# Expert output product in fp32r parts instead of fp32, with two scaled-output buffers

## The chip, the core and the metric

The kernel runs on one core of a Trainium2 chip. The metric is the device time of one execution in microseconds (us). The core has five engines that run side by side, each through its own list of instructions in a fixed order: TensorE (PE in the rows; PEld is its weight load), VectorE (DVE), ScalarE (ACT), GpSimd (POOL) and SyncE (SP), which here only starts transfers. They wait for each other and for DMA transfers by semaphores.

## The reference, cut to what matters

Two layers; each mixes tokens by attention and a recurrent scan, and then sends its 1024 tokens through a mixture of 32 experts, two of them per token:

```python
def block_mlp(args):
    tok, e = args
    xb = h_pad[tok]                                      # up to 128 tokens of expert e
    hid = jax.nn.silu(xb @ w_gate[e]) * (xb @ w_up[e])   # 1024 -> 256
    return hid @ w_down[e]                               # 256 -> 1024: the output product
...
y = jax.ops.segment_sum(yb.reshape(R, D) * row_w[:, None], row_tok, num_segments=T + 1)
```

## The kernel before, in words

Each layer has a mixing part and then the expert loop in `moe`, which handles 35 blocks of 128 rows in turn (32 experts and three slots for experts with more than 128 rows). Only this loop is changed. Each expert e goes through these steps:

- **Gather** (GpSimd, L1614): 128 token rows are fetched by index into one of two `xg`.
- **Prepare** (L1625): TensorE turns the rows in eight transposes into PSUM; ScalarE casts them to `xT_hi` (fp32r), and VectorE subtracts that from the PSUM values, which leaves the second part `xT_lo`.
- **Weights**: SyncE loads the 1 MB halves of `w_gu`, two per expert, into raw buffers (`RAW` of them), and the 1 MB `w_d` into one of three. For each half, `split` (L1591) has ScalarE cast it to `w_hi` and VectorE subtract to get `w_lo`, all 128x2048; three pairs of buffers hold the parts.
- **Up** (L1640): 24 matmuls, for each of eight slices hi x hi, lo x hi and hi x lo, into `h_ps`.
- **Hidden** (L1634): tanh on ScalarE, two VectorE instructions on `th` (128x256).
- **Turned** (L1663): two transposes of `th`, and a ScalarE copy to `hT`.
- **Down** (L1682): the output product in plain fp32, `hT` by `w_d`, four matmuls in the program that run as eight passes on TensorE, into `y_ps`; VectorE scales the result by the token's weight and the gate `gt2` into `yo` (L1673), of which there is one buffer.
- **Scatter** (GpSimd, L1676): `yo` goes by index to rows of `yd` in memory.

`in_order` pins the order of the loop's instructions on TensorE, ScalarE, VectorE and GpSimd to that of the program: in turn e these are `up`(e), the first split of a half, `turned`(e-1), `prepare`(e+1), `gather`(e+3), `hidden`(e), then `down`(e-1), `scatter`(e-1) and the second split. SyncE's loads are issued in program order with waits for the buffers. `route_overflow` (the tables for experts with more rows; `ro_or` on VectorE, `ro_pv` on TensorE) isn't pinned: a scheduler mixes it into the first turns of the loop. Everything else in the program is ordered by the scheduler too.

Of the kernel before, what the change touches and what calls it, by code (L numbers as in the profile page):

```python
# [10 lines left out]
F32 = mybir.dt.float32  # L11
F32R = mybir.dt.float32r
# [3 lines left out]
OP = mybir.AluOpType  # L16
# [4 lines left out]
T = 1024  # L21
D = 1024
# [30 lines left out]
class Trunk:  # L53
# [1516 lines left out]
        self.raw = [wp.tile([128, 4, 512], F32, name=f"w_gu{i}") for i in range(2)]  # L1570
        self.wd = [wp.tile([128, 2, D], F32, name="w_d0")]

    RAW = 5

    def more_tiles(self, wp):
        self.parts = [[wp.tile([128, 4, 512], F32R, name=f"w_{n}{i}") for n in ("hi", "lo")] for i in range(3)]
# [9 lines left out]
        self.nc.sync.dma_start(self.raw[n % self.RAW], self.expert_source(l, e, "moe_w_gu")[n % 2])  # L1586

    def load_d(self, l, i, e):
        self.nc.sync.dma_start(self.wd[i % 3], self.expert_source(l, e, "moe_w_down"))

    def split(self, raw, parts, eng):  # L1591

# [3 lines left out]

    def split_half(self, n, eng=None):
        self.split(self.raw[n % self.RAW], self.parts[n % 3], eng or self.nc.vector)

    def moe(self, l, side, psum):  # L1600

        nc, tc = self.nc, self.tc
        with ExitStack() as s:
            xp, tx = s.enter_context(self.pool(name="xE", bufs=2, side=side)), self.tx
            gt2 = tx.tile([128, D], F32, name="gt2", tag="v2", bufs=1)
# [1 line left out]
            for x in xg:  # L1607
                nc.gpsimd.memset(x, 0.0)
            ths = tx.tile([128, 2, 256], F32, name="th", tag="mt")
            hT = tx.tile([128, 2, 128], F32, name="hT", tag="mt")  # L1610
            scat = []

            def gather(e):
# [11 lines left out]
            def prepare(e):  # L1625

                pt = transposed(e)
                hi = tx.tile([128, 8, 128], F32R, name="xT_hi", tag="hl")
                lo = xp.tile([128, 8, 128], F32R, name="xT_lo", tag="xT_lo")
                nc.scalar.copy(hi, pt)  # L1630
                nc.vector.tensor_tensor(lo, pt, hi.bitcast(F32), op=OP.subtract)  # L1631
                return hi, lo

            def hidden(e, ph):  # L1634
                th = ths[:, e % 2]
                nc.scalar.activation(th, ph[:, 0:256], AF.Tanh, scale=0.5)
                nc.vector.scalar_tensor_tensor(th, th, 1.0, ph[:, 0:256], op0=OP.add, op1=OP.mult)
                nc.vector.tensor_mul(th, th, ph[:, 256:512])
# [21 lines left out]
                    nc.tensor.matmul(ph, x[:, k, :], self.raw[(2 * e + k // 4) % self.RAW][:, k % 4, :], start=(k == 0), stop=(k == NK - 1))  # L1660
                hidden(e, ph)

            def turned(e):  # L1663
                pt = psum.tile([128, 2, 128], F32, name="hT_ps", tag="hT", bufs=1)
                for k in range(2):
                    nc.tensor.transpose(pt[:, k, :], ths[:, e % 2, 128 * k:128 * k + 128], self.ident)
                nc.scalar.copy(hT, pt)

            yos = {}

            def scaled(e, po):
                yo = yos[e] = tx.tile([128, D], F32, name="yo", tag="x", bufs=1)
                nc.vector.scalar_tensor_tensor(yo, po, self.wsl[:, e:e + 1], gt2, op0=OP.mult, op1=OP.mult)  # L1673

            def scatter(e):
                st = nc.gpsimd.indirect_dma_start(out=self.yd, out_offset=bass.IndirectOffsetOnAxis(ap=self.idx_s[:, e:e + 1], axis=0),  # L1676
                                                  in_=yos.pop(e), in_offset=None, bounds_check=2 * T - 1, oob_is_err=False)
                for o in scat:
                    tc.declare_no_dep(st.ins, o.ins, reason="every slot holds another row")
                scat.append(st)  # L1680

            def down(e):  # L1682
                w = self.wd[e % 3]
# [17 lines left out]
            N = 32 + self.MORE_E  # L1701
# [8 lines left out]
            for e in range(N):  # L1710
                with self.in_order(last):
                    ph = up(e, x)
                    if e + 1 < N:
                        self.split_half(2 * e + 3)
                    if e:
                        turned(e - 1)
                    if e + 1 < N:
                        x = prepare(e + 1)
                    if e + 3 < N:
                        gather(e + 3)  # L1720
                    hidden(e, ph)
                if e == 0:
                    nc.sync.dma_start(gt2, self.mod_row(l, 5).partition_broadcast(128))
                with self.in_order(last):
                    if e:
                        down(e - 1)
                        scatter(e - 1)
                    if e + 2 < N:
                        self.split_half(2 * e + 4)
                for n in (2 * e + 8, 2 * e + 9):  # L1730
                    if n < 2 * N:
                        self.load_gu(l, n, expert(n // 2))
                if e and e + 2 < N:
# [9 lines left out]
            with ExitStack() as ifs:  # L1743
                for b in range(self.MORE_E, 15):
                    ifs.enter_context(tc.If(n > b))
                    if b == self.MORE_E:
                        gather(32 + b)
                        overflow(b)
                    x = prepare_late(32 + b)
                    if b + 1 < 15:  # L1750
                        gather(33 + b)
                        overflow(b + 1)
                    up_late(32 + b, x)
                    turned(32 + b)
                    down(32 + b)
                    scatter(32 + b)

    def sum_of(self, t, pool):

# [35 lines left out]
    def layer(self, l, x_src):  # L1795

        nc = self.nc
        here, there = "left", "right"
        self.use_params(l)
        self.l = l  # L1800
        self.h2d = self.dram.tile([T, D], F32, name=f"h2d{l}")
        self.yd = self.dram.tile([2 * T, D], F32, name=f"yd{l}")
        self.ad = [self.dram.tile([128, 4, D], F32, name=f"ad{l}{g}") for g in range(2)]
        self.phase_a(l, x_src, self.psum, here, there)
        if l == 0 and "mixed" in self.dbg:
            [nc.sync.dma_start(self.dbg["mixed"][:, 4 * g:4 * g + 4], self.ad[g]) for g in range(2)]
        se = ExitStack()
        self.first_tiles(se.enter_context(self.pool(name=f"wF{l}", bufs=1, side=there)))

        def more():  # L1810

            self.wo_stack.close()
            self.more_tiles(se.enter_context(self.pool(name=f"wE{l}", bufs=1, side=here)))
            for n in range(2, 4):
                self.load_gu(l, n, n // 2)
            for n in range(3):
                self.split_half(n, nc.gpsimd)
            for n in range(4, 8):
                self.load_gu(l, n, n // 2)

        with ExitStack() as s:
            psum = Banks(**{n: s.enter_context(self.pool(name=f"ps{n}e{l}", bufs=b, space=PSUM))
                            for n, b in (("tp", 2), ("po", 4), ("pl", 2))})
            self.out_proj(l, there, psum, lambda: (self.load_gu(l, 0, 0), self.load_gu(l, 1, 0), self.load_d(l, 0, 0)), more)
        if l == 0:
            self.dump("xm", self.xm)
        with ExitStack() as s:
            psum = s.enter_context(self.pool(name=f"psE{l}", bufs=1, space=PSUM))
            wp = s.enter_context(self.pool(name=f"wD{l}", bufs=1, side=here))
            self.wd += [wp.tile([128, 2, D], F32, name=f"w_d{i}") for i in range(1, 3)]  # L1830
# [117 lines left out]
```

## Time and profile before

| | |
|---|---|
| median of 3 runs | 2877.4 us (2875.11 to 2880.29) |
| the profiled execution | 2878.6 us, span 2876.6 us |
| granted TensorE clock, mean over the span | 0.904 |
| TensorE matmul busy | 2426.0 us (84%) |
| VectorE busy | 1862.8 us (65%) |
| ScalarE busy | 1108.6 us (39%) |
| GpSimd busy | 875.3 us (30%) |

The span is the time from the first to the last instruction in the profile. Busy shares are means over parts of the program with different limits; the changed loop takes about 375 us of the span in each layer and has to be read by itself.

### The profile page before, as it was taken

Reading aid. Unit: us, or ns where it says so; the run is one execution under the profiler, and the core shown is the slowest. Engines: PE = TensorE matmul, PEld = TensorE weight load, DVE = VectorE, ACT = ScalarE, POOL = GpSimd, SP = SyncE. Lnnn points to the kernel's source line nnn. Section 1 sums busy time; section 2 is a strip of 40 time slices with the busy share of each in tenths; the row PEclk is TensorE's granted clock in tenths of the full one; section 3 lists DMA queues with packets and bytes.
Section 4 is the critical chain, followed back from the end, with each engine's and each line's share of the span. In section 5 each row is a group of like instructions: output and inputs, shape, how many; then the busy total and the mean of one; then the engine's idle time right before and its main releaser. Section 6 shows DMA issues by size and latency. Waiting matters only on the chain.

```text
span 2876.6 us, 45429 instructions
## 1 busy us (share of the span) xinstructions
PE 2426.0 (84%) x17313; PEld 1847.9 (64%) x17313; DVE 1862.8 (65%) x3875; ACT 1108.6 (39%) x1988; POOL 875.3 (30%) x565
## 2 busy tenths in 40 slices
PE   5998997999789689998669878999878986988991
PEld 3766665777678666665447666777766775655660
DVE  5367775555684767666465787756567567656765
ACT  3333332343362244444243333334345332444541
POOL 4122232221420524444322212222232032334432
PEclk8999987998899789999889878889878986999996
DMA  8486674452532468888533333554444225888964
GB/s 285 152 256 208 198 228 127 134 151 88 187 103 89 162 237 312 318 321 326 196 126 109 108 103 124 167 149 125 119 150 125 88 110 177 324 300 299 330 247 187
DMA packets 262789, 542.70 MB, mean 189 GB/s; under 512 B 76376, under 2 KB 180768, under 8 KB 232608
## 3 DMA queue, kind: packets, MB, share of 16 engines
q1 hardware_dynamic: 234560, 484.61, 50.1%
q0 software_dynamic: 23376, 40.99, 3.9%
q10 hardware_dynamic: 4624, 14.06, 1.2%
q8 instruction: 142, 2.33, 0.3%
q14 instruction: 87, 0.71, 0.1%
HBM read 459.29 MB, written 120.09 MB: 201 GB/s over the span
## 4 chain that ended last, share of the span: by engine, by line
PE 40%; issue 20%; DVE 19%; DMA 10%; POOL 7%; ACT 3%; SPq 1%; POOLq 0%; DVEq 0%; ACTq 0%
PE pj L350 5%; PE pj L352 4%; PE pj L351 4%; POOL xg L1614 4%; POOL yd L1676 2%; DMA sp_z<-z 2%; DVE sv_t L741 2%; DVE sv_m L739 2%; PE po L1299 2%; PE at_o L1196 2%; PE po L1300 2%; PE po L1301 2%; DMA yd<-yo,idx_s 1%; DMA ada_w<-in_ada_w 1%; PE rb_y L899 1%
## 5 line engine op out<-in xcount | busy, mean ns | idle before, releaser
L1594 ACT CAST w_hi<-w_gu 128x2048 fp32r<-128x2048 f32 x140 | 266.8, 1907 | 283.8 <-PE h_ps L1647 279.7
L350 PE MATMUL pj<-hh,wa_hi 128*128 128x512 f32 x800 | 340.7, 426 | 2.4 <-ACT wa_hi L337 1.7
L351 PE MATMUL pj<-hl,wa_hi 128*128 128x512 f32 x800 | 331.3, 414 | 1.4 <-DVE hl L327 1.3
L352 PE MATMUL pj<-hh,wa_lo 128*128 128x512 f32 x800 | 327.5, 411 | 3.2 <-POOL wa_lo L338 3.2
L1676 POOL DMA_INDIRECT yd<-yo,idx_s x70 | 183.6, 2623 | 445.1 <-DVE yo L1673 425.6
L1595 DVE TENSOR_TENSOR w_lo<-w_gu,w_hi 128x2048 fp32r<-128x2048 f32 x134 | 301.6, 2284 | 20.2 <-ACT w_hi L1594 20.2
L1647 PE MATMUL h_ps<-w_hi,xT_lo 128*128 128x512 f32 x560 | 225.2, 402 | 54.7 <-DVE xT_lo L1631 54.6
L1687 PE MATMUL y_ps<-w_d,hT 128*128 128x512 f32 x560 | 254.3, 597 | 13.0 <-issue 5.8
L1673 DVE SCALAR_TENSOR_TENSOR yo<-y_ps,wsl,gt 128x1024 f32<-128x1024 f32 x70 | 89.9, 1284 | 237.5 <-DMA yd<-yo,idx_s 199.0
L1646 PE MATMUL h_ps<-w_hi,xT_hi 128*128 128x512 f32 x560 | 243.5, 435 | 0.0
L1648 PE MATMUL h_ps<-w_lo,xT_hi 128*128 128x512 f32 x560 | 220.2, 393 | 0.0
L338 POOL TENSOR_TENSOR wa_lo<-wa_raw,wa_hi 128x1024 fp32r<-128x1024 f32 x50 | 120.9, 2417 | 308.3 <-ACT wa_hi L337 237.4
L350 PEld LDWEIGHTS pj<-hh,wa_hi 128*128 128x128 f32 x800 | 157.7, 197 | 41.5 <-issue 6.0
L351 PEld LDWEIGHTS pj<-hl,wa_hi 128*128 128x128 f32 x800 | 157.2, 196 | 39.0 <-issue 5.2
L352 PEld LDWEIGHTS pj<-hh,wa_lo 128*128 128x128 f32 x800 | 156.9, 196 | 39.1 <-POOL wa_lo L338 4.4
L1687 PEld LDWEIGHTS y_ps<-w_d,hT 128*128 128x128 f32 x560 | 101.0, 190 | 117.3 <-issue 108.2
L1647 PEld LDWEIGHTS h_ps<-w_hi,xT_lo 128*128 128x128 f32 x560 | 105.8, 189 | 106.6 <-DVE xT_lo L1631 84.4
L1614 POOL DMA_INDIRECT xg<-h2d,idx_g x70 | 119.9, 1713 | 89.3 <-PE ro_pv L1564 49.7
L1646 PEld LDWEIGHTS h_ps<-w_hi,xT_hi 128*128 128x128 f32 x560 | 106.3, 190 | 33.3 <-issue 12.9
L1167 DVE TENSOR_REDUCE at_mx<-at_s 128x1 f32<-128x256 f32 (+7 forms) x128 | 95.9, 752 | 38.4 <-PE at_s L1165 37.5
L1648 PEld LDWEIGHTS h_ps<-w_lo,xT_hi 128*128 128x128 f32 x560 | 105.8, 189 | 20.5
L1169 ACT ACTIVATE at_p<-at_s,at_mx 128x256 f32<-128x256 f32 (+7 forms) x128 | 94.9, 743 | 62.3 <-DVE at_mx L1167 61.7
(435 smaller groups left out, 5389.8 us busy)
## 6 DMA issues: line engine op xcount, KB each, us to landing
w_gu<-in_moe_w_gu SPq DMA_DIRECT2D x140, 1024.0 KB
w_d<-in_moe_w_down SPq DMA_DIRECT2D x70, 1024.0 KB
ada_w<-in_ada_w SPq DMA_DIRECT2D x80, 512.0 KB
wa_raw<-in_w_in SPq DMA_DIRECT2D x50, 512.0 KB
sp_z<-z SPq DMA_DIRECT2D x32, 768.0 KB
b_zz<-sp_z SPq DMA_DIRECT2D x32, 512.0 KB
cy<-yd SPq DMA_DIRECT2D x16, 1024.0 KB
qkv<-qst SPq DMA_DIRECT2D x48, 256.0 KB
```

Source lines behind the costliest of these rows:

```text
L338: nc.gpsimd.tensor_tensor(lo, raw, hi.bitcast(F32), op=OP.subtract)
L350: nc.tensor.matmul(ps, hi[:, k, :], self.hh[k][:, sl], start=(k == 0), stop=False)
L351: nc.tensor.matmul(ps, hi[:, k, :], self.hl[k][:, sl], start=False, stop=False)
L352: nc.tensor.matmul(ps, lo[:, k, :], self.hh[k][:, sl], start=False, stop=(k == NK - 1))
L1594: self.nc.scalar.copy(hi, raw)
L1595: eng.tensor_tensor(lo, raw, hi.bitcast(F32), op=OP.subtract)
L1614: nc.gpsimd.indirect_dma_start(out=xg[e % 2], out_offset=None, in_=self.h2d, in_offset=bass.IndirectOffsetOnAxis(ap=self.idx_g[:, e:e + 1] ...
L1646: nc.tensor.matmul(ph, hi[:, k, :], whi[:, k % 4, :], start=(k == 0), stop=False)
L1647: nc.tensor.matmul(ph, lo[:, k, :], whi[:, k % 4, :], start=False, stop=False)
L1648: nc.tensor.matmul(ph, hi[:, k, :], wlo[:, k % 4, :], start=False, stop=(k == NK - 1))
L1676: st = nc.gpsimd.indirect_dma_start(out=self.yd, out_offset=bass.IndirectOffsetOnAxis(ap=self.idx_s[:, e:e + 1], axis=0), in_=yos.pop(e), ...
L1687: nc.tensor.matmul(po[:, 512 * half:512 * half + 512], hT[:, k, :], w[:, k, 512 * half:512 * half + 512], start=(k == 0), stop=(k == 1))
```

## The change

The output product of the pinned loop is made as the products of `up` are: both sides are given in two parts of type fp32r, and three products are summed (hi x hi, lo x hi, hi x lo).

- `turned` now has ScalarE write the first part of `hT` and VectorE subtract it from the PSUM values for the second part.
- `split_d` is new: ScalarE casts `w_d` to `w_dh` (two buffers), and GpSimd subtracts to get `w_dl` (one buffer). The cast for e comes after `hidden`(e), the subtraction for e after `down`(e-1) and ahead of `scatter`(e-1).
- `yo` has two buffers, taken in turn. `xT_lo` has one instead of two, the raw buffers are four instead of five, `w_d` two instead of three; the loads move accordingly. The next `w_d` load waits for `split_d` instead of the matmuls.
- The blocks behind the pinned loop (which this input doesn't reach) keep the plain fp32 product as `down_late`.

```diff
-    RAW = 5
+    RAW = 4
...
-        self.nc.sync.dma_start(self.wd[i % 3], self.expert_source(l, e, "moe_w_down"))
+        self.nc.sync.dma_start(self.wd[i % 2], self.expert_source(l, e, "moe_w_down"))
...
+    def split_d(self, i, part):
+        hi = self.wdh[i % 2]
+        if part == 0:
+            self.nc.scalar.copy(hi, self.wd[i % 2])
+        else:
+            self.nc.gpsimd.tensor_tensor(self.wdl, self.wd[i % 2], hi.bitcast(F32), op=OP.subtract)
...
-            hT = tx.tile([128, 2, 128], F32, name="hT", tag="mt")
+            hT = tx.tile([128, 2, 2, 128], F32R, name="hT", tag="mt")
...
-                lo = xp.tile([128, 8, 128], F32R, name="xT_lo", tag="xT_lo")
+                lo = xp.tile([128, 8, 128], F32R, name="xT_lo", tag="xT_lo", bufs=1)
...
+            def turned(e):
+
+                pt = hidden_turned(e)
+                nc.scalar.copy(hT[:, 0], pt)
+                nc.vector.tensor_tensor(hT[:, 1], pt, hT[:, 0].bitcast(F32), op=OP.subtract)
+
+            yos = [p.tile([128, D], F32, name="yo", tag="x", bufs=1) for p in (tx, xp)]
...
-                yo = yos[e] = tx.tile([128, D], F32, name="yo", tag="x", bufs=1)
-                nc.vector.scalar_tensor_tensor(yo, po, self.wsl[:, e:e + 1], gt2, op0=OP.mult, op1=OP.mult)
+                nc.vector.scalar_tensor_tensor(yos[e % 2], po, self.wsl[:, e:e + 1], gt2, op0=OP.mult, op1=OP.mult)
...
-                w = self.wd[e % 3]
+                whi, wlo = self.wdh[e % 2], self.wdl
+                po = psum.tile([128, D], F32, name="y_ps", tag="y", bufs=1)
+                hi, lo = hT[:, 0], hT[:, 1]
+                for n, (x, w) in enumerate(((hi, whi), (lo, whi), (hi, wlo))):
+                    for half in range(2):
+                        cs = slice(512 * half, 512 * half + 512)
+                        for k in range(2):
+                            nc.tensor.matmul(po[:, cs], x[:, k, :], w[:, k, cs], start=(n + k == 0), stop=(n + k == 3))
+                scaled(e, po)
...
                     hidden(e, ph)
+                    self.split_d(e, 0)
...
                     if e:
                         down(e - 1)
+                    self.split_d(e, 1)
+                    if e:
                         scatter(e - 1)
...
-                for n in (2 * e + 8, 2 * e + 9):
+                for n in (2 * e + 7, 2 * e + 8):
                     if n < 2 * N:
                         self.load_gu(l, n, expert(n // 2))
-                if e and e + 2 < N:
+                if e + 2 < N:
                     self.load_d(l, e + 2, expert(e + 2))
```

GpSimd in the middle of layer 0's loop, before (L1614 is the gather, L1676 the scatter):

```order
L1614 DMA xg0_10477<-h2d0_614,idx_g_10451 128x1024
L1676 DMA yd0_615<-yo_12003,idx_s_10450 2048x1024
L1614 DMA xg1_10478<-h2d0_614,idx_g_10451 128x1024
L1676 DMA yd0_615<-yo_12068,idx_s_10450 2048x1024
L1614 DMA xg0_10477<-h2d0_614,idx_g_10451 128x1024
```

The same place of the changed kernel (L1605 is the subtraction of `split_d`, L1688 the scatter, L1621 the gather):

```order
L1605 TENSOR_TENSOR w_dl_10468<-w_d0_9797,w_dh0_10469 128x2048
L1688 DMA yd0_615<-yo_10483,idx_s_10448 2048x1024
L1621 DMA xg0_10476<-h2d0_614,idx_g_10449 128x1024
L1605 TENSOR_TENSOR w_dl_10468<-w_d1_10467,w_dh1_10470 128x2048
L1688 DMA yd0_615<-yo_10482,idx_s_10448 2048x1024
L1621 DMA xg1_10477<-h2d0_614,idx_g_10449 128x1024
```

Each turn now has one subtraction into the only `w_dl`, ahead of the scatter.

VectorE at such a place, before (L1673 is `yo`, L1595 the subtraction for `w_lo`, L1631 `xT_lo`, L1637 and L1638 `th`):

```order
L1673 SCALAR_TENSOR_TENSOR yo_12393<-y_ps_12388,wsl_10452,gt2_10476 128x1024
L1595 TENSOR_TENSOR w_lo1_10325<-w_gu3_10329,w_hi1_10324 128x2048
L1595 TENSOR_TENSOR w_lo2_10327<-w_gu4_10330,w_hi2_10326 128x2048
L1631 TENSOR_TENSOR xT_lo_12444<-xT_ps_12434,xT_hi_12443 128x1024
L1637 SCALAR_TENSOR_TENSOR th_10481<-th_10481,h_ps_12403 128x256
```

And in the changed kernel (L1680 is the second part of `hT`, L1685 `yo`):

```order
L1595 TENSOR_TENSOR w_lo2_10327<-w_gu2_10328,w_hi2_10326 128x2048
L1595 TENSOR_TENSOR w_lo0_10323<-w_gu3_10329,w_hi0_10322 128x2048
L1680 TENSOR_TENSOR hT_10481<-hT_ps_12404,hT_10481 128x256
L1638 TENSOR_TENSOR xT_lo_12419<-xT_ps_12409,xT_hi_12418 128x1024
L1644 SCALAR_TENSOR_TENSOR th_10480<-th_10480,h_ps_12377 128x256
L1645 TENSOR_TENSOR th_10480<-th_10480,h_ps_12377 128x256
L1685 SCALAR_TENSOR_TENSOR yo_10483<-y_ps_12429,wsl_10450,gt2_10475 128x1024
```

The new `hT` row stands behind both `w_lo`, and both stand behind `yo`, as before.

TensorE between two products `up`, before (L1666 turns `th`, L1622 the next expert's rows, L1687 is the output product) and in the changed kernel (L1673, L1629, L1702):

```order
L1666 MATMUL hT_ps<-ident,th 128x128 x2
L1622 MATMUL xT_ps<-ident,xg_10478 128x128 x8
L1687 MATMUL y_ps<-w_d_10469,hT 128x512 x4
```

```order
L1673 MATMUL hT_ps<-ident,th 128x128 x2
L1629 MATMUL xT_ps<-ident,xg_10477 128x128 x8
L1702 MATMUL y_ps<-w_dh_10470,hT 128x512 x8
L1702 MATMUL y_ps<-w_dl,hT 128x512 x4
```

The four matmuls become twelve; the last four read `w_dl`.

## Rows read from the trace of the kernel before

**Rows 1.** Timeline, VectorE: start us, length us, line, operation, tiles, [idle before <-releaser].
```profile
1042.69 1.28 DVE L1673 SCALAR_TENSOR_TENSOR yo<-y_ps,wsl,gt 128x1024 f32<-128x1024 f32 x1 [0.61 <-PE y_ps L1687]
...
1383.21 1.28 DVE L1673 SCALAR_TENSOR_TENSOR yo<-y_ps,wsl,gt 128x1024 f32<-128x1024 f32 x1 [5.05 <-PE hT_ps L1666]
...
1417.13 1.28 DVE L1673 SCALAR_TENSOR_TENSOR yo<-y_ps,wsl,gt 128x1024 f32<-128x1024 f32 x1 [5.72 <-PEq L1743]
...
2434.94 1.28 DVE L1673 SCALAR_TENSOR_TENSOR yo<-y_ps,wsl,gt 128x1024 f32<-128x1024 f32 x1 [0.61 <-PE y_ps L1687]
...
2784.78 1.28 DVE L1673 SCALAR_TENSOR_TENSOR yo<-y_ps,wsl,gt 128x1024 f32<-128x1024 f32 x1 [4.01 <-DMA yd<-yo,idx_s]
...
2818.22 1.28 DVE L1673 SCALAR_TENSOR_TENSOR yo<-y_ps,wsl,gt 128x1024 f32<-128x1024 f32 x1 [5.24 <-DMA yd<-yo,idx_s]
```

**Rows 2.** Waits, 1060 to 1330 us: who <- for whom: us, times, longest.
```profile
DVE yo L1673 <- DMA yd<-yo,idx_s: 83.5, 23, 4.8
...
PEld h_ps L1647 <- DVE xT_lo L1631: 31.0, 20, 2.2
```

**Rows 3.** Timeline, VectorE and GpSimd, one expert in layer 0.
```profile
1222.74 1.28 DVE L1673 SCALAR_TENSOR_TENSOR yo<-y_ps,wsl,gt 128x1024 f32<-128x1024 f32 x1 [4.07 <-DMA yd<-yo,idx_s]
1223.94 4.48 DVE L1595 TENSOR_TENSOR w_lo<-w_gu,w_hi 128x2048 fp32r<-128x2048 f32 x2
1228.34 1.22 DVE L1631 TENSOR_TENSOR xT_lo<-xT_ps,xT_hi 128x1024 fp32r<-128x1024 f32 x1
1229.48 0.41 DVE L1637 SCALAR_TENSOR_TENSOR th<-th,h_ps 128x256 f32<-128x256 f32 x1
...
1234.24 1.28 DVE L1673 SCALAR_TENSOR_TENSOR yo<-y_ps,wsl,gt 128x1024 f32<-128x1024 f32 x1 [3.90 <-DMA yd<-yo,idx_s]
...
1224.30 2.80 POOL L1676 DMA_INDIRECT yd<-yo,idx_s  x1 [6.66 <-DVE yo L1673]
```

**Rows 4.** Timeline, TensorE's matmuls, the same expert.
```profile
1223.50 0.38 PE L1666 MATMUL hT_ps<-ident,th 128*128 128x128 f32 x2
...
1224.59 3.60 PE L1687 MATMUL y_ps<-w_d,hT 128*128 128x512 f32 x8
...
1229.61 0.50 PE L1647 MATMUL h_ps<-w_hi,xT_lo 128*128 128x512 f32 x1 [1.19 <-DVE xT_lo L1631]
...
1231.33 0.39 PE L1648 MATMUL h_ps<-w_lo,xT_hi 128*128 128x512 f32 x1
...
1234.96 0.38 PE L1666 MATMUL hT_ps<-ident,th 128*128 128x128 f32 x2
```

**Rows 5.** Timeline, the start and the end of layer 0's loop.
```profile
1030.93 1.90 ACT L1594 CAST w_hi<-w_gu 128x2048 fp32r<-128x2048 f32 x1
...
1401.76 0.98 POOL L1676 DMA_INDIRECT yd<-yo,idx_s  x1 [6.70 <-DVE yo L1673]
...
1405.50 0.38 PE L1666 MATMUL hT_ps<-ident,th 128*128 128x128 f32 x2
...
1406.39 3.70 PE L1687 MATMUL y_ps<-w_d,hT 128*128 128x512 f32 x8 [0.52 <-ACT hT L1667]
```

**Rows 6.** Stretch, length, busy of PE, PEld, DVE, ACT, POOL, clock, DMA share, GB/s.
```profile
1060.00:1330.00 270.00, 249.52 (x1027) 170.96 (x1027) 182.11 (x155) 131.08 (x123) 109.89 (x48) 1.00 0.87 320
```

**Rows 7.** Timeline, VectorE and GpSimd ahead of layer 0's loop (`wo`: output projection's weights).
```profile
758.25 1.22 DVE L1223 TENSOR_TENSOR wo_raw<-wo_raw,gt 128x1024 f32<-128x1024 f32 x1
...
761.65 3.37 DVE L1223 TENSOR_TENSOR wo_raw<-wo_raw,gt 128x1024 f32<-128x1024 f32 x1
...
760.62 3.32 POOL L1225 TENSOR_TENSOR wo_lo<-wo_raw,wo_hi 128x1024 fp32r<-128x1024 f32 x1 [3.01 <-ACT wo_hi L1224]
...
976.29 4.50 POOL L1595 TENSOR_TENSOR w_lo<-w_gu,w_hi 128x2048 fp32r<-128x2048 f32 x1
```

**Rows 8.** Timeline, GpSimd and VectorE in layer 0's mixing part (`pj` lies in PSUM).
```profile
350.60 2.36 POOL L338 TENSOR_TENSOR wa_lo<-wa_raw,wa_hi 128x1024 fp32r<-128x1024 f32 x1
...
350.69 0.75 DVE L368 SCALAR_TENSOR_TENSOR krv<-pj,pv,krv 128x511 f32<-128x511 f32 x1 [2.89 <-ACT krv L367]
```

More of the change, by code (lines that the diff above doesn't have):

```diff
@@ L1661, in up_late, with hidden_turned @@
                 hidden(e, ph)
-            def turned(e):
+            def hidden_turned(e):
                 pt = psum.tile([128, 2, 128], F32, name="hT_ps", tag="hT", bufs=1)
@@ L1666, in turned @@
                     nc.tensor.transpose(pt[:, k, :], ths[:, e % 2, 128 * k:128 * k + 128], self.ident)
-                nc.scalar.copy(hT, pt)
-            yos = {}
+                return pt
+            def turned(e):
[3 more added lines that the diff above has]
+            yos = [p.tile([128, D], F32, name="yo", tag="x", bufs=1) for p in (tx, xp)]
             def scaled(e, po):
-                yo = yos[e] = tx.tile([128, D], F32, name="yo", tag="x", bufs=1)
-                nc.vector.scalar_tensor_tensor(yo, po, self.wsl[:, e:e + 1], gt2, op0=OP.mult, op1=OP.mult)
+                nc.vector.scalar_tensor_tensor(yos[e % 2], po, self.wsl[:, e:e + 1], gt2, op0=OP.mult, op1=OP.mult)
             def scatter(e):
                 st = nc.gpsimd.indirect_dma_start(out=self.yd, out_offset=bass.IndirectOffsetOnAxis(ap=self.idx_s[:, e:e + 1], axis=0),
-                                                  in_=yos.pop(e), in_offset=None, bounds_check=2 * T - 1, oob_is_err=False)
+                                                  in_=yos[e % 2], in_offset=None, bounds_check=2 * T - 1, oob_is_err=False)
                 for o in scat:
@@ L1682, in down, with down_late @@
             def down(e):
-                w = self.wd[e % 3]
+                whi, wlo = self.wdh[e % 2], self.wdl
[7 more added lines that the diff above has]
+                scaled(e, po)
+            def down_late(e):
+                pt = hidden_turned(e)
+                hT = ths[:, 1 - e % 2].rearrange("p (a b) -> p a b", a=2)
+                nc.vector.tensor_copy(hT, pt)
+                w = self.wd[e % 2]
                 po = psum.tile([128, D], F32, name="y_ps", tag="y", bufs=1)
@@ L1689, in down @@
                 scaled(e, po)
+                scatter(e)
             def block_weights(b):
@@ L1753, in moe @@
                     up_late(32 + b, x)
-                    turned(32 + b)
-                    down(32 + b)
-                    scatter(32 + b)
+                    down_late(32 + b)
     def sum_of(self, t, pool):
@@ L1817, in more @@
                 self.split_half(n, nc.gpsimd)
-            for n in range(4, 8):
+            for n in range(4, 7):
                 self.load_gu(l, n, n // 2)
@@ L1829, in layer @@
             wp = s.enter_context(self.pool(name=f"wD{l}", bufs=1, side=here))
-            self.wd += [wp.tile([128, 2, D], F32, name=f"w_d{i}") for i in range(1, 3)]
-            for e in (1, 2):
-                self.load_d(l, e, e)
+            self.wd += [wp.tile([128, 2, D], F32, name="w_d1")]
+            self.wdl = wp.tile([128, 2, D], F32R, name="w_dl")
+            self.wdh = [wp.tile([128, 2, D], F32R, name=f"w_dh{i}") for i in range(2)]
+            self.load_d(l, 1, 1)
             self.moe(l, there, psum)
```

## Prediction

> **What bounds the kernel now.** I read the page first, for the place: the change touches only the loop over experts, which runs once per layer. I then took VectorE's timeline at the first, the 31st and the last scaled output `yo` of each layer's 35 experts. From the first to the last it is 1417.13 - 1042.69 = 374.4 us in layer 0 and 2818.22 - 2434.94 = 383.3 us in layer 1, so 757.7 us of the span; over the first 30 intervals an expert costs 340.5 / 30 = 11.35 and 349.8 / 30 = 11.66 us, 11.5 in the mean [rows 1].
>
> The list of waits says why. In 270 us of layer 0 (24 experts), VectorE waits 83.5 us, in 23 of them, before `yo` for the scatter of the expert before to land, and TensorE's weight load waits 31.0 us for `xT_lo`, which VectorE makes later [rows 2]. One expert on VectorE shows the ring [rows 3]: `yo` at 1222.74, its scatter at 1224.30, and the next `yo` at 1234.24, as the single `yo` buffer only comes free when the scatter has landed. Behind the waiting `yo` stand two `w_lo` (4.48 us together) and `xT_lo`, without which TensorE can't go on: it starts its waiting matmul at 1229.61, 0.05 after `xT_lo` has ended at 1229.56. TensorE's own work is less [rows 4]: 1.1 us for ten transposes (1223.50 to 1224.59), 3.6 for the eight passes of the output product with the drain of the last, and 24 matmuls of 0.23 (23 from 1229.61 to 1234.96), 5.5 us; together 10.2 us. So the ring over the landing sets about 11.5, with TensorE 1.3 us below it.
>
> **The change part by part.** *Removed: the wait on the landing.* With two `yo` buffers a `yo` waits for the scatter two experts back, over 20 us earlier; the ring took 11.5 us from one `yo` to the next [rows 3]. This wait goes entirely.
>
> *TensorE.* Eight passes become twelve matmuls at 0.23: 3.6 us become 2.9 with the drain, and TensorE's work falls to 9.5 us [rows 4].
>
> *ScalarE* gets one 128x2048 cast, 1.90 us [rows 5]. With two such casts, `xT_hi`, tanh and `hT` it had 131 us of work in those 270, 5.5 us per expert [rows 6]; 7.4 stay under 11. The cast stands between tanh and the cast for the first `w_lo`, which VectorE can't begin before the end of `yo` anyway. I cost it at nothing; uncovered, it would cost 1.9 us per expert.
>
> *VectorE* gets `hT_lo` (128x256 from PSUM). A `th` of that size ends 0.33 us after the instruction ahead of it (1229.89 against 1229.56) [rows 3].
>
> *GpSimd* gets the subtraction `w_dl`, 128x2048: 4.50 us, the price of the same subtraction on GpSimd in the prologue [rows 7]. This is the term that decides, because of where it stands and what it excludes.
>
> What it excludes: in [rows 7] VectorE's 128x1024 product of two SBUF tiles takes 1.22 us alone, but 3.37 when a GpSimd subtraction runs: it starts at 761.65, GpSimd's ends at 760.62 + 3.32 = 763.94, and VectorE's ends 1.08 us later, at 765.02. So it did nothing until GpSimd was done, and then ran for its own 1.07 us. VectorE's instruction with one input in PSUM isn't held: 0.75 us beside a GpSimd subtraction that began 0.09 us earlier [rows 8], so `yo`, `xT_lo`, `hT_lo` and `th` go on. `w_lo` has both inputs in SBUF, and must take turns with `w_dl`. The Trainium skill says the same in "SBUF — State Buffer", section "Who interferes with whom": a VectorE instruction with two SBUF inputs contends with a GpSimd one that reads SBUF, and the loser blocks for the whole instruction. It speaks against this change, and the trace agrees (3.37 us for 1.22).
>
> Where it stands: `w_dl` has one buffer, so the subtraction for expert e starts when the last matmul of the output product of e-1 has read it; call that moment D. `yo`(e-1) waits for D too, and both `w_lo` stand behind `yo` on VectorE. So GpSimd always comes first by the length of `yo`, and a new ring closes:
> - D to the start of `w_dl`: between the 0.05 of TensorE after `xT_lo` [rows 4] and the 0.28 from the end of `yo` (1224.02) to its scatter [rows 3]; I take 0.12.
> - `w_dl`: 4.50 [rows 7].
> - first `w_lo`, held until then: 2048 elements where 1024 took 1.08 after the release, about 2.15 [rows 7]; the second 4.48 - 2.28 = 2.20 [rows 3].
> - `hT_lo`, which stands behind both: 0.33 [rows 3].
> - TensorE's last eight matmuls, four with `hT_lo` and four with `w_dl`, up to the next D. In [rows 4] the matmul that waited for `xT_lo` began 0.05 after its end, and the eighth from there at 1231.33, 0.39 long: 0.05 + (1231.33 - 1229.61) + 0.39 = 2.16.
>
> Sum: 0.12 + 4.50 + 2.15 + 2.20 + 0.33 + 2.16 = 11.46 us per expert, against 11.5. One ring replaces another of the same length, and this one doesn't shrink where landings are short.
>
> The pieces differ at both ends. Start: the first `w_dl` follows the cast put at 1030.93 [rows 5]; 1030.93 + 1.90 + 11.46 = 1044.3 for the first D and `yo`, against 1042.69 [rows 1]: +1.6 per layer. From there D to D holds for experts 1 to 32: 32 x 11.46 = 366.7. Expert 33 has no `w_lo` ahead of it: 24 matmuls (5.5), turned `hT` until the product starts 0.9 [rows 5], 2.8 for the product, 0.3 to its end: 9.5. Expert 34 needs its `w_dl` after the D of 33: 0.12 + 4.50 and four matmuls, 1.2: 5.8. Then 382.0 per layer from first to last `yo`.
>
> *Moved.* The routing's small instructions (`ro_or`, `ro_pv`) are pinned nowhere, and the order now has seven `ro_or` of some 0.2 us per layer between `yo` and `hT_lo`, inside the ring, and three `ro_pv` of about 0.2 on TensorE ahead of the last matmuls: +2 us per layer (estimate; below 0, above 6).
>
> *Smaller buffers.* Four raw buffers for five and two `w_d` for three: those 270 us ran at 320 GB/s with the DMA engines 87% busy, so 86.4 MB, 3.6 per expert [rows 6]. At 11.46 us per expert 314 GB/s are wanted. A raw buffer has two turns, 22.9 us; from its cast to the end of `w_lo` it is held up to 1.9 + 4.5 + 2.2 = 8.6, which leaves 14.3 us for a load, where three take 10. Nothing added; the bound above is 10 us if the first loads lag. The scheduler also reorders some of layer 1's mixing, between the two loops: 0, plus or minus 6.
>
> *Sum:* 2 x (382.0 + 1.6 + 2.0) = 771.2 against 757.7: +13.5 us. The profiled execution took 2878.6 us (span 2876.6), 1.2 above the median 2877.4 of three; so 2892 for it, 2891 for the median.
>
> **Rivals.**
> *Faster, no turns taken.* If `w_dl` and `w_lo` ran side by side, the ring would be TensorE's 9.5 us or the transfers': 87% of 270 us over 24 experts is 9.8 us at full use [rows 6]. At 10.2 per expert a layer takes 32 x 10.2 + 15.3 = 341.7, two 683, or 74 us less: 2803. Against it stands [rows 7].
> *Ring shorter than summed.* Each 0.1 us of the ring is 6.4 us. At 11.25 (0.2 less, if the matmuls' modelled ends or the releases are earlier) the time is 2878, no change; at 11.1 it is faster. For it: the latencies of 0.05 to 0.28 are read from single rows.
> *Longer, GpSimd late.* If GpSimd isn't free within the 1.3 us of `yo` after D, the first `w_lo` goes ahead, `w_dl` then waits 2.2 us, and the second `w_lo` follows: about 1.3 + 2.2 + 4.5 + 2.2 + 0.33 + 2.16 = 12.7. In one expert of four that adds 20 us: 2911; in all, 2970. GpSimd's last work before D is scatter and gather: the scatter takes 2.80 us from a start just after `w_lo` began [rows 3] and 0.98 with no `w_lo` running [rows 5]: the first `w_lo` ended at about 1226.14, and 0.97 later the scatter was done, so it waited that `w_lo` out. Put into the ring, the gather ends some 1.4 us before D. The same section of the Trainium skill infers that such a `tensor_tensor` doesn't hold up descriptor making, which needs only the write interface; the trace has 2.80 against 0.98, and the measurement decides. By the rule GpSimd would be free some 3 us before D and this rival would all but vanish, with the sum unchanged.
>
> **How the numbers follow.** The ring as summed: 0.66, 2891, its own range 2882 to 2902. Shorter ring: 0.18, some two thirds of it within no change. Side by side: 0.05. GpSimd or loads late: 0.11. About 0.2%, 5.8 us, is what a measurement of this kernel can tell from no change. Faster by more takes the 0.05 and about 0.07 of the shorter ring: 0.12. Within: the rest of the shorter ring and the low edge of the first: 0.16. Slower: 0.72. The range 2868 to 2916 leaves out the side-by-side case, the shortest rings and late GpSimd in more than a third of the experts.
>
> **What would show it.** `w_lo` in two kinds, one of about 2.2 us and one of 4 to 5.5 that ends some 2.15 after `w_dl`; `w_dl` at 4.50; no wait of `yo` on a landing; TensorE waiting about 2 us for `hT_lo` after its first four matmuls of the output product; 11.4 to 11.6 us per expert, alike in both layers, with a granted clock of 1.00 throughout. I am wrong if `w_lo` stays at 2.28 throughout (side by side), if `w_dl` itself takes 6 us or more (order turned), if ScalarE's casts wait for loads, or if the time between the two loops differs by more than 6 us.

## The result, and the profile after

The changed kernel takes 2945.45 us (median of 4 runs, 2939.81 to 2951.21), the kernel before 2876.26 (4 runs) beside it: a ratio of 1.0241 with a 95% interval of 1.0215 to 1.0268. It is slower, as forecast, but by 69 us where 13.5 were summed, and 2945 lies outside the range of 2868 to 2916.

| profiled execution | before | after |
|---|---|---|
| span | 2876.6 us | 2938.0 us |
| granted TensorE clock, mean | 0.904 | 0.888 |
| VectorE busy | 1862.8 us | 2110.0 us |
| GpSimd busy | 875.3 us | 1215.6 us |
| loops, first to last `yo`, both layers | 757.7 us | 826.1 us |

The last line comes from VectorE's timeline, which answers to [rows 1]:

```profile
1458.56 1.28 DVE L1685 SCALAR_TENSOR_TENSOR yo<-y_ps,wsl,gt 128x1024 f32<-128x1024 f32 x1 [4.44 <-PE y_ps L1702]
...
2468.99 1.28 DVE L1685 SCALAR_TENSOR_TENSOR yo<-y_ps,wsl,gt 128x1024 f32<-128x1024 f32 x1
...
2878.84 1.28 DVE L1685 SCALAR_TENSOR_TENSOR yo<-y_ps,wsl,gt 128x1024 f32<-128x1024 f32 x1 [4.42 <-PE y_ps L1702]
```

The first `yo` of layer 0 starts at 1042.32, so the loops take 416.2 and 409.9 us: 68.4 more than before, of a span that is 61.4 longer. The 32 turns from one D to the next that the prediction put at 11.46 us take 12.53 in layer 0 and 12.33 in layer 1 in the mean. They are not alike: 23 of the 64 take less than 11.8, most of them 11.70 to 11.75, and the others up to 13.6. The medians are 69.2 us apart and the spans only 61.4, mainly because the profiled execution of the changed kernel is the shortest of its four (2939.8 us).

Stretches of the changed kernel, with the columns of [rows 6], show the first sign of the cause: the granted clock, 1.00 before, is 0.91 and 0.92. Two neighbouring turns (11.70 and 13.05 us), and one of the last of layer 1, stand below, and then the last eight matmuls of each of the two neighbours.

```profile
1060.00:1330.00 270.00, 229.01 (x1003) 182.89 (x1002) 246.72 (x164) 155.94 (x131) 201.55 (x65) 0.91 0.76 286
2470.00:2740.00 270.00, 232.04 (x1032) 185.68 (x1031) 251.54 (x169) 157.21 (x132) 206.35 (x66) 0.92 0.78 298
1216.77:1228.47 11.70, 10.22 (x47) 8.18 (x47) 11.38 (x7) 6.80 (x6) 9.37 (x3) 0.95 0.67 251
1228.47:1241.52 13.05, 10.91 (x47) 8.69 (x46) 11.39 (x7) 7.55 (x7) 9.40 (x3) 0.88 0.82 315
2840.21:2851.95 11.74, 9.60 (x47) 7.72 (x46) 11.39 (x7) 7.29 (x7) 7.51 (x2) 1.00 0.78 300
1226.32:1228.44 2.12, 2.12 (x9) 1.78 (x10) 1.83 (x3) 2.12 (x2) 0.50 (x1) 1.00 1.02 429
1238.04:1241.49 3.45, 3.45 (x9) 2.73 (x10) 1.82 (x3) 1.85 (x2) 0.49 (x1) 0.56 1.00 405
```

The timeline of the changed kernel over the end of the fast turn and the slow one, VectorE, GpSimd and the output product on TensorE, with two matmuls of `up` (L1653) from the fast turn's start:

```profile
1228.47 1.28 DVE L1685 SCALAR_TENSOR_TENSOR yo<-y_ps,wsl,gt 128x1024 f32<-128x1024 f32 x1 [0.29 <-PE y_ps L1702]
1229.67 7.97 DVE L1595 TENSOR_TENSOR w_lo<-w_gu,w_hi 128x2048 fp32r<-128x2048 f32 x2
1237.57 0.41 DVE L1680 TENSOR_TENSOR hT<-hT_ps,hT 128x256 fp32r<-128x256 f32 x1
...
1228.68 4.62 POOL L1605 TENSOR_TENSOR w_dl<-w_d,w_dh 128x2048 fp32r<-128x2048 f32 x1 [1.86 <-PE y_ps L1702]
1233.45 2.88 POOL L1688 DMA_INDIRECT yd<-yo,idx_s  x1 [0.15 <-issue]
...
1216.53 0.63 PE L1653 MATMUL h_ps<-w_hi,xT_hi 128*128 128x512 f32 x1
...
1218.58 0.39 PE L1653 MATMUL h_ps<-w_hi,xT_hi 128*128 128x512 f32 x1
...
1226.32 1.19 PE L1702 MATMUL y_ps<-w_dh,hT 128*128 128x512 f32 x4 [1.48 <-DVE hT L1680]
1227.36 1.08 PE L1702 MATMUL y_ps<-w_dl,hT 128*128 128x512 f32 x4
...
1234.73 1.17 PE L1702 MATMUL y_ps<-w_dh,hT 128*128 128x512 f32 x4
1238.04 1.74 PE L1702 MATMUL y_ps<-w_dh,hT 128*128 128x512 f32 x4 [2.14 <-DVE hT L1680]
1239.58 1.91 PE L1702 MATMUL y_ps<-w_dl,hT 128*128 128x512 f32 x4
```

The ring is there, link by link. `yo` starts 0.03 us after D (1227.36 + 1.08 = 1228.44) and waits for no landing; `w_dl` starts 0.24 after D and takes 4.62; the two `w_lo` that took 4.48 in [rows 3] take 7.97 and end 4.34 after `w_dl` (1237.64 against 1233.30), and what they stand still counts as busy in the table above; `hT_lo` ends 0.34 later, at 1237.98. All this is the same in fast and slow turns. What differs stands behind it: the eight matmuls that followed `hT_lo` took 2.1 us in the fast turn (1226.32 to 1228.44) and 3.45 in the slow one (1238.04 to 1241.49). A group of four spans 1.91 us instead of 1.08. The granted clock over these eight is 0.56 in the slow turn, so TensorE was at the lower of its two levels, 1.2 instead of 2.4 GHz, for most of them; over the fast turn's eight it is 1.00. Ahead of the eight of the slow turn TensorE had waited 2.14 us for `hT_lo`.

The eight matmuls account for all that differs between turns. In the 58 of the 64 turns in which TensorE's timeline lists this wait, a turn less its eight matmuls is 9.46 to 9.90 us, and 9.56 to 9.61 in 53 of them. The eight take 2.11 to 2.15 us in all 23 fast turns and up to 3.69 in the others; what they take over 2.12 adds up to about 38 us. The waits go with it: 1.79 to 2.44 us in the 35 longer turns, but 0.88 to 1.76 in 18 of the 23 fast turns. Each of these 18 follows a longer turn, whose lower level still holds for the first matmuls of `up` (0.63 us instead of 0.39, hence the 0.95 of the fast turn above), so that TensorE comes to its wait later.

The list of waits of the same 270 us as [rows 2] shows how often (PEld is the wait as TensorE's weight load has it, PE as its matmuls have it):

```profile
PEld y_ps L1702 <- DVE hT L1680: 44.4, 19, 2.9
PE y_ps L1702 <- DVE hT L1680: 36.3, 19, 2.4
...
DVE yo L1685 <- PE y_ps L1702: 20.7, 20, 1.9
```

The theory for the experiments: the ring with its turns between GpSimd and VectorE takes 11.70 us where 11.46 were summed; and TensorE's wait brings its clock to the lower level, just for the matmuls that close the ring. Rivals: the matmuls are slow for another reason; no turns are taken; or GpSimd's subtraction costs as much wherever `hT_lo` stands.

### The profile page after: what moved, and what is told of

Same layout as the page of the kernel before. It is cut to its first block, busy times and chain, and to the rows that moved or that the text cites. A ratio compares the mean times of both kernels' runs of the same rounds, so it can differ in the third digit from the quotient of the medians.

```text
span 2938.0 us, 46381 instructions
## 1 busy us (share of the span) xinstructions
PE 2430.9 (83%) x17593; PEld 1933.0 (66%) x17593; DVE 2110.0 (72%) x3945; ACT 1234.4 (42%) x2058; POOL 1215.6 (41%) x635
## 4 chain that ended last, share of the span: by engine, by line
PE 24%; DVE 17%; DMA 4%; issue 2%; ACT 2%; POOL 1%; SPq 0%; DVEq 0%; ACTq 0%; POOLq 0%
DVE w_lo L1595 7%; PE y_ps L1702 3%; PE pj L350 2%; PE pj L351 2%; PE pj L352 2%; PE h_ps L1653 1%; PE h_ps L1654 1%; PE h_ps L1655 1%; DVE sv_m L739 1%; PE po L1299 1%; PE po L1300 1%; PE po L1301 1%; PE at_o L1196 1%; DMA sp_z<-z 1%; DVE sv_t L741 1%
## 5 line engine op out<-in xcount | busy, mean ns | idle before, releaser
L1595 DVE TENSOR_TENSOR w_lo<-w_gu,w_hi 128x2048 fp32r<-128x2048 f32 x134 | 498.2, 3756 | 16.0 <-ACT w_hi L1594 16.0
L1605 POOL TENSOR_TENSOR w_dl<-w_d,w_dh 128x2048 fp32r<-128x2048 f32 x70 | 322.9, 4612 | 186.9 <-PE y_ps L1702 155.3
L1702 PE MATMUL y_ps<-w_dh,hT 128*128 128x512 f32 x560 | 180.0, 448 | 113.3 <-DVE hT L1680 109.9
L1653 PE MATMUL h_ps<-w_hi,xT_hi 128*128 128x512 f32 x560 | 231.6, 414 | 0.0
L1702 PEld LDWEIGHTS y_ps<-w_dh,hT 128*128 128x128 f32 x560 | 100.9, 200 | 154.5 <-DVE hT L1680 135.7
L1688 POOL DMA_INDIRECT yd<-yo,idx_s x70 | 191.1, 2729 | 15.7 <-issue 12.3
L1621 POOL DMA_INDIRECT xg<-h2d,idx_g x70 | 127.3, 1818 | 67.7 <-PE ro_pv L1564 25.6
L1685 DVE SCALAR_TENSOR_TENSOR yo<-y_ps,wsl,gt 128x1024 f32<-128x1024 f32 x70 | 89.9, 1284 | 71.7 <-PE y_ps L1702 71.3
L922 POOL TENSOR_TENSOR b_y<-b_y,b_lnx 128x512 f32<-128x512 f32 x16 | 20.6, 1286 | 284.0 <-issue 162.7
L1603 ACT CAST w_dh<-w_d 128x2048 fp32r<-128x2048 f32 x70 | 133.1, 1902 | 0.0
L1653 PEld LDWEIGHTS h_ps<-w_hi,xT_hi 128*128 128x128 f32 x560 | 114.6, 205 | 26.2
```

Source lines behind the costliest of these rows:

```text
L1595: eng.tensor_tensor(lo, raw, hi.bitcast(F32), op=OP.subtract)
L1603: self.nc.scalar.copy(hi, self.wd[i % 2])
L1605: self.nc.gpsimd.tensor_tensor(self.wdl, self.wd[i % 2], hi.bitcast(F32), op=OP.subtract)
L1653: nc.tensor.matmul(ph, hi[:, k, :], whi[:, k % 4, :], start=(k == 0), stop=False)
L1702: nc.tensor.matmul(po[:, cs], x[:, k, :], w[:, k, cs], start=(n + k == 0), stop=(n + k == 3))
```

## The experiments

Every ratio is to the kernel before, run on the same chip. The kernel before had a median of 2883.4 us (13 runs) beside the first product three times, `w_dl` on VectorE, `turned` earlier and the two `yo`, and of 2871.3 (12 runs) beside the other four, so the ratios are not quotients of the medians in this table. As the code outside the loops took 2103 to 2125 us in the profiled executions of these kernels, turns and loops (both layers, first to last `yo`) are compared as well.

| kernel | loops, us | median, us | ratio (95%) |
|---|---|---|---|
| before | 757.7 | 2876.3 | 1 |
| changed | 826.1 | 2945.5 | 1.0241 (1.0215 to 1.0268) |
| first product three times | 788.5 | 2912.7 | 1.0135 (1.0083 to 1.0186) |
| first product twice | 785.6 | 2900.6 | 1.0097 (1.0071 to 1.0124) |
| `w_dl` on VectorE | 702.0 | 2816.7 | 0.9793 (0.9743 to 0.9843) |
| `w_dl` half and half | 702.1 | 2815.8 | 0.9795 (0.9745 to 0.9845) |
| `turned` earlier | 734.3 | 2855.6 | 0.9925 (0.9896 to 0.9954) |
| `w_dl` on VectorE, `turned` earlier | 679.3 | 2807.8 | 0.9760 (0.9705 to 0.9815) |
| before, with two `yo` | 675.6 | 2802.2 | 0.9757 (0.9710 to 0.9805) |
| changed, with one `yo` | 861.4 | 2970.8 | 1.0329 (1.0270 to 1.0387) |

**TensorE's wait filled with matmuls.** In `down`, ahead of the three products:

```diff
+                for _ in range(2):
+                    for half in range(2):
+                        cs = slice(512 * half, 512 * half + 512)
+                        for k in range(2):
+                            nc.tensor.matmul(po[:, cs], hi[:, k, :], whi[:, k, cs], start=(k == 0), stop=(k == 1))
```

> The changed kernel, with the first four matmuls of the output product (first part by first part) issued three times instead of once; the repeats overwrite the same sums, so the result is the same, and TensorE has 1.9 us more to do in the 2.1 us in which it waits for the second part of hT. Theory (the idle lowers the granted clock): the eight matmuls behind hT_lo take 2.2 us in every expert instead of 2.2 to 3.7, an expert takes 11.70 us throughout, the granted clock of the loop is back at 1.00, and the 46.9 us that the 64 long intervals of the changed kernel have over 64 x 11.70 are gone: about 2898. Rival (those matmuls are slow for another reason, operands or transfers): the repeats lie in the idle time, the intervals still reach 13 us, about 2945. Second rival (the clock stays low anyway): the repeats run at half rate too, 3.7 us for 2.1 of idle, and the time rises over 2960.

The second kernel of this kind has `range(1)`.

> The changed kernel, with the first four matmuls of the output product issued twice (in the first filled kernel three times), so that TensorE's wait for hT_lo goes from 2.1 to 1.2 us instead of 0.2. Theory (only a wait of about 2 us brings the clock down; the kernel before kept 1.00 with waits of 1.55 in the mean): 11.70 us throughout and a clock of 1.00, about 2905 against a kernel before of 2876. Rival (any wait lowers it, in proportion): half of the 46.9 us comes back, intervals still reach 13 us: about 2922.

More work made the changed kernel faster (ratio 1.0241, with one repeat 1.0097, with two 1.0135). With two repeats, the same 270 us, and then the timeline of one turn's output product (L1702 are the repeats, L1707 the product):

```profile
1060.00:1330.00 270.00, 263.29 (x1257) 213.64 (x1255) 262.79 (x172) 163.81 (x138) 215.94 (x69) 1.00 0.81 305
```

```profile
1233.18 2.10 PE L1702 MATMUL y_ps<-w_dh,hT 128*128 128x512 f32 x8
1235.12 1.07 PE L1707 MATMUL y_ps<-w_dh,hT 128*128 128x512 f32 x4
1236.49 1.19 PE L1707 MATMUL y_ps<-w_dh,hT 128*128 128x512 f32 x4 [0.30 <-DVE hT L1680]
1237.52 1.08 PE L1707 MATMUL y_ps<-w_dl,hT 128*128 128x512 f32 x4
```

The same two views with one repeat:

```profile
1060.00:1330.00 270.00, 243.00 (x1163) 195.97 (x1162) 262.71 (x174) 164.40 (x138) 215.80 (x70) 1.00 0.81 305
```

```profile
1243.22 1.20 PE L1707 MATMUL y_ps<-w_dh,hT 128*128 128x512 f32 x4 [1.20 <-DVE hT L1680]
1244.25 1.07 PE L1707 MATMUL y_ps<-w_dl,hT 128*128 128x512 f32 x4
```

The clock is 1.00 in both, and from the sixth turn on nearly every turn takes 11.70 to 11.75 us, with 0.30 or 1.20 us of waiting left. Over the 64 turns one repeat gives back 795.65 - 753.35 = 42.3 us. That is less than the 46.9 expected mainly because the first five turns, with the routing's `ro_or` in them, keep about 1.5 us a layer over 11.70 (2 with two repeats). Two repeats give back 41.7, and cost 4 us in the two tails, where no wait covers them; their 2912.7 us miss the 2898 expected. The rivals of these two runs are out: the eight matmuls have the operands that they had before, and run at full rate.

**`w_dl` on VectorE, and half of it there.**

```diff
-            self.nc.gpsimd.tensor_tensor(self.wdl, self.wd[i % 2], hi.bitcast(F32), op=OP.subtract)
+            self.nc.vector.tensor_tensor(self.wdl, self.wd[i % 2], hi.bitcast(F32), op=OP.subtract)
```

> The changed kernel, with the subtraction w_dl on VectorE instead of GpSimd, at the same place in the order (behind yo, ahead of both w_lo). Theory (turns between GpSimd and VectorE make the ring long): yo 1.28, w_dl 2.24, two w_lo 4.48, hT_lo 0.33 and eight matmuls 2.2 close a ring of 10.5 us, in which VectorE works almost all the time; 64 x (12.43 - 10.5) = 124 us less, about 2822 if the clock stays up. If TensorE's wait for hT_lo (about 1 us) still lowers the clock, up to 0.8 us per expert more: 2870. Rival (no turns are taken; w_lo was long for another reason): VectorE only gets 2.24 us more per expert, and the time rises by up to 64 x 2.2 us over 2945.

```diff
+            for k, eng in enumerate((self.nc.gpsimd, self.nc.vector)):
+                eng.tensor_tensor(self.wdl[:, k], self.wd[i % 2][:, k], hi[:, k].bitcast(F32), op=OP.subtract)
```

> The changed kernel with w_dl cut in two 128x1024 halves: GpSimd subtracts one, VectorE the other, behind yo and ahead of both w_lo. Theory (VectorE's instructions with two SBUF inputs wait out GpSimd's subtraction): 0.24 + 2.33 until GpSimd is done, then 1.1 for VectorE's half, 4.48 for two w_lo, 0.33 for hT_lo and 2.2 for eight matmuls: 10.65 us per expert, with TensorE's wait down to 1.0 us and the clock at 1.00; about 2831. Rival (side by side, no turns): 1.28 + 1.12 + 4.48 + 0.33 + 2.2 = 9.4, less than the 9.8 of the transfers: about 2780.

All of it on VectorE, one turn, VectorE and then the output product on TensorE:

```profile
1185.40 1.28 DVE L1685 SCALAR_TENSOR_TENSOR yo<-y_ps,wsl,gt 128x1024 f32<-128x1024 f32 x1 [0.28 <-PE y_ps L1702]
1186.61 2.28 DVE L1605 TENSOR_TENSOR w_dl<-w_d,w_dh 128x2048 fp32r<-128x2048 f32 x1
1188.80 4.49 DVE L1595 TENSOR_TENSOR w_lo<-w_gu,w_hi 128x2048 fp32r<-128x2048 f32 x2
...
1193.68 1.20 PE L1702 MATMUL y_ps<-w_dh,hT 128*128 128x512 f32 x4 [0.85 <-DVE hT L1680]
```

Half and half, VectorE and GpSimd:

```profile
1179.96 1.28 DVE L1686 SCALAR_TENSOR_TENSOR yo<-y_ps,wsl,gt 128x1024 f32<-128x1024 f32 x1 [0.29 <-PE y_ps L1703]
1181.16 2.26 DVE L1606 TENSOR_TENSOR w_dl<-w_d,w_dh 128x1024 fp32r<-128x1024 f32 x1
1183.34 4.48 DVE L1595 TENSOR_TENSOR w_lo<-w_gu,w_hi 128x2048 fp32r<-128x2048 f32 x2
...
1179.93 2.40 POOL L1606 TENSOR_TENSOR w_dl<-w_d,w_dh 128x1024 fp32r<-128x1024 f32 x1 [1.63 <-PE y_ps L1703]
```

The turns are 10.43 and 10.40 us, and the granted clock is 1.00 in both over 1060 to 1330 us. The two `w_lo` are back at 4.48. VectorE's half takes as long (2.26) as the whole does alone (2.28): it waits until GpSimd is done at 1182.33 and then needs 1.09. So the two engines take turns at this size too, 9.4 us side by side is out, and here VectorE gains nothing by what GpSimd takes over of the subtraction. The Trainium skill, in "SBUF — State Buffer", section "Who interferes with whom", calls the shared path an exclusive lock for a whole instruction; these rows agree.

**`turned` earlier**, without and with `w_dl` on VectorE:

```diff
+                    if e:
+                        turned(e - 1)
                     ph = up(e, x)
                     if e + 1 < N:
                         self.split_half(2 * e + 3)
-                    if e:
-                        turned(e - 1)
```

> The changed kernel, with turned(e-1) one step earlier in the pinned order: ahead of up(e) instead of behind it, so that TensorE's transposes stand right behind the last output product and hT_lo stands between the two w_lo on VectorE. GpSimd's w_dl stays and still holds the w_lo up. Theory (the ring runs through hT_lo because it stands behind both w_lo): the ring over w_dl then closes over xT_lo into the product up after next, two turns for about 20 us, so 10.0 us per expert with TensorE at 9.6 and the transfers at 9.8; 10.2 for 64 intervals that now take 12.43 in the mean: 143 us less, about 2803. Rival (w_dl itself is the price, wherever hT_lo stands): GpSimd's 4.62 and the two w_lo stay in one chain with the yo, 11.4 or more per expert: 2880 or more.

> Both edits that shortened the ring together: w_dl on VectorE, and turned(e-1) ahead of up(e). Theory (with w_dl on VectorE its own work is the bound, not the chain through hT_lo): VectorE was busy 262.5 of 270 us at 10.43 us per expert, so 10.15 is left when hT_lo no longer waits for anything: 64 x 0.28 = 18 us less than with w_dl on VectorE alone (2817), about 2799. Rival (the chain through hT_lo set the 10.43): TensorE's 9.5 or the transfers' 9.8 would show, 40 us less: 2777.

With GpSimd's `w_dl`, two turns of VectorE, and the `w_dl` of the first:

```profile
1173.74 1.28 DVE L1685 SCALAR_TENSOR_TENSOR yo<-y_ps,wsl,gt 128x1024 f32<-128x1024 f32 x1
1174.93 4.66 DVE L1595 TENSOR_TENSOR w_lo<-w_gu,w_hi 128x2048 fp32r<-128x2048 f32 x1
1179.51 0.41 DVE L1680 TENSOR_TENSOR hT<-hT_ps,hT 128x256 fp32r<-128x256 f32 x1
1179.85 2.28 DVE L1595 TENSOR_TENSOR w_lo<-w_gu,w_hi 128x2048 fp32r<-128x2048 f32 x1
...
1183.96 1.28 DVE L1685 SCALAR_TENSOR_TENSOR yo<-y_ps,wsl,gt 128x1024 f32<-128x1024 f32 x1
1185.72 5.08 DVE L1595 TENSOR_TENSOR w_lo<-w_gu,w_hi 128x2048 fp32r<-128x2048 f32 x1 [0.48 <-ACT w_hi L1594]
...
1172.81 4.62 POOL L1605 TENSOR_TENSOR w_dl<-w_d,w_dh 128x2048 fp32r<-128x2048 f32 x1
```

Both expectations missed: 10.2 and 11.2 us in turn, later 10.45 and 10.95, so 10.7 for two neighbours, and 734.3 us for the loops. Over all 64 turns the mean is 11.0, as the first of each layer take up to 15.3; why these are so long stays open. Moving `hT_lo` does open the ring, which the rival denied. But the hold stays: `w_lo` takes 4.66 and 5.08 for 2.28, and with these 2.4 to 2.8 us VectorE has hardly any idle time left in the first of the turns (0.1 us at most between its instructions from 1173.74 to 1183.96) and 0.48 before the first `w_lo` in the second. I had summed the ring over TensorE and not VectorE's own turn. With `w_dl` on VectorE too, the turn is 10.05 us, and VectorE is busy 269 of 270:

```profile
1060.00:1330.00 270.00, 256.18 (x1245) 206.97 (x1244) 269.05 (x226) 189.23 (x161) 123.77 (x54) 1.00 0.96 358
```

That is the bound that was named (VectorE's work), 10.05 where 10.15 was worked out.

**One part of the change alone.** The kernel before with two `yo`, the second in the room of the second `xT_lo`:

```diff
-                lo = xp.tile([128, 8, 128], F32R, name="xT_lo", tag="xT_lo")
+                lo = xp.tile([128, 8, 128], F32R, name="xT_lo", tag="xT_lo", bufs=1)
...
-            yos = {}
+            yos = [p.tile([128, D], F32, name="yo", tag="x", bufs=1) for p in (tx, xp)]
...
-                yo = yos[e] = tx.tile([128, D], F32, name="yo", tag="x", bufs=1)
+                yo = yos[e % 2]
...
-                                                  in_=yos.pop(e), in_offset=None, bounds_check=2 * T - 1, oob_is_err=False)
+                                                  in_=yos[e % 2], in_offset=None, bounds_check=2 * T - 1, oob_is_err=False)
```

> The kernel before, with two yo buffers instead of one (the second in the room of the second xT_lo) and nothing else. Theory (the ring over the landing set the 11.5 us): yo no longer waits for a landing, and an expert takes TensorE's own 10.2 us, with the transfers at 9.8: 64 x 1.3 = 83 us less than before, about 2793. Rival (w_lo and xT_lo on VectorE set the pace anyway): the wait moves to another place and the time stays within 10 us of 2876.

And the changed kernel with one: `for p in (tx,)] * 2`.

> The changed kernel with one yo buffer instead of two. Theory (in the changed kernel the second buffer is worth nothing, because the ring over w_dl is the longer one): the scatter stands behind w_dl on GpSimd, so it starts 4.8 us after D, and it takes 2.7 us and some 7 more to land; yo then runs about 3 us after D and ends before w_dl does, so VectorE's w_lo begin when they did. 11.8 us at a clock of 1.00, 12.4 to 12.6 with the present clock: 2945 to 2960. Rival (the landing closes a ring of its own through yo): 4.8 + 2.7 + 7.1 from yo to yo, 14.7 us per expert, 145 us more: 3090.

The same 270 us of the kernel before with two `yo`:

```profile
1060.00:1330.00 270.00, 270.00 (x1144) 191.41 (x1143) 209.56 (x171) 143.83 (x135) 101.52 (x54) 1.00 0.99 358
```

TensorE works without a break, 10.02 us per turn, and the loops are 82.1 us shorter (83 expected). Its loops are the shortest of all; its whole time can't be told from that of `w_dl` on VectorE with `turned` earlier (0.9757 against 0.9760). Put on top of it, the rest of the change costs 826.1 - 675.6 = 150.5 us in the loops. With one `yo` in the changed kernel a turn takes 12.9 us in the mean, irregular between 10.5 and 16.2, and the waits from 1060 to 1330 us show both rings at work:

```profile
DVE yo L1685 <- DMA yd<-yo,idx_s: 84.0, 20, 5.3
...
PEld y_ps L1702 <- DVE hT L1680: 48.9, 19, 3.7
```

So the second `yo` buffer isn't worth nothing there, as I had expected, but 35.3 us in the loops (861.4 against 826.1). The 14.7 us ring of the rival, over the landing alone, isn't there either.

## Why the prediction was right in direction and wrong in size

- **What bounded the kernel before, and the removed wait on the landing**: right. With two `yo` alone a turn takes 10.02 us, near the 10.2 summed for TensorE, and in the changed kernel VectorE's list of waits names the landing no more.
- **Turns between `w_dl` and `w_lo`, GpSimd first**: right (the start of `w_dl` lies 0.51 us behind that of `yo` at most). Side by side and GpSimd late are both out, and the loads weren't late either: no wait of ScalarE's casts for one is listed. In the first four turns of each layer it is the routing's `ro_or`, put at 0.2 us and standing ahead of the `w_lo`, that waits `w_dl` out, so both `w_lo` then take their 4.48:

```profile
1055.39 3.71 DVE L1563 TENSOR_SCALAR ro_or<-r_io,ro_rm 128x128 f32<-128x128 f32 x1
```

- **The ring's length**: mis-sized by 0.24 us. D to the start of `w_dl` is 0.24 instead of 0.12, and `w_dl` takes 4.62 instead of 4.50; with 4.34 for both `w_lo`, 0.34 for `hT_lo` and 2.16 at full clock that is 11.70. Over 64 turns 15.4 us.
- **The step that failed** is the last term, "TensorE's last eight matmuls ... 2.16", with "a granted clock of 1.00 throughout". I took 2.16 from rows at a clock of 1.00, and forecast in the same text that TensorE would wait about 2 us ahead of these matmuls. Waits and clock were treated as two things. The runs show one: with the wait of 2.1 us the clock is 0.91 to 0.92 over 270 us and the eight matmuls take up to 3.69; with the wait filled down to 1.20 or 0.30 the clock is 1.00, and the difference is 42.3 us, 0.66 a turn in the mean. No rival had it. The Trainium skill has a case of this kind in "TensorE: Matmul & The Clock Gate", section "HAM oscillation — how this bites in real kernels": a loop that waits some 3 to 5 us for a transfer in each turn finds its matmuls at the lower clock again and again. The trace agrees as to the matmuls behind the wait (1.91 us for 1.08), but it shows them slow after waits of 2.1 us, shorter than the page's, and not in every turn.
- **The ends and the routing**: the last two turns took 9.2 and 6.05 (9.5 and 5.8 summed), the routing 1.5 to 2 us per layer, read from the filled kernels, where 2 were put. The first `yo` of layer 0 came 0.4 us earlier, not 1.6 later, and the time between the loops fell from 1017.8 to 1010.4, by 7.4 where more than 6 was named as a sign of error; kernels that change nothing there had 999 to 1021, so no cause is read from it.

The sum, mended: 13.5 + 15.4 for the ring + 42.3 for the clock + 0.4 for routing and ends - 10.2 outside the loops (-7.0 where 3.2 were put) = 61.4, the growth of the profiled span.

## What to carry to other kernels

Where a change makes TensorE wait in every turn, price the matmuls behind that wait at both levels of the clock, above all if they close the ring; repeats of a matmul that lie in the wait show within one run what the clock costs. The subtraction of two SBUF tiles was not taken off VectorE here by giving it to GpSimd, since VectorE's own such instructions stood still meanwhile; look for that before counting on it. And run each part of a change alone: here two `yo` buffers gave 82 us in the loops, and the rest of the change took that back and 68 more.

## What the hardware showed unexpectedly

- A wait of 2.1 us per turn of some 12 brought TensorE to the lower clock; 1.20 did not, nor did the waits of the kernel before for `xT_lo`, with a clock of 1.00 [rows 6]. Counted at the matmuls, as 2.1 and 1.20 are, these are 1.31 us in the mean and 1.6 at most; the 1.55 of the expectation above is counted at the weight load [rows 2], where the changed kernel has 44.4 / 19 = 2.3:

```profile
PE h_ps L1647 <- DVE xT_lo L1631: 19.6, 15, 1.6
```

- Not every such wait did it: from 2840.21 on the waits are 2.14 and 2.12 and the clock is 1.00. Five of the 23 fast turns have waits of 1.98 to 2.14; what tells these from the longer turns is open.
- `w_dl` took 4.62 us in the ring, 4.54 where no `w_lo` waited for it (the last expert), and 4.50 in the prologue [rows 7].
